# A 31-column loop of fp32 matmuls with its two operands exchanged

## Chip, cores and metric

The kernel runs on one core of a Trainium2 chip. The metric is the device time of one execution in microseconds (us), here the median of several runs of the same program. The engines are TensorE (PE in the profile, with its weight loads on a row of their own, PEld), VectorE (DVE), ScalarE (ACT), GpSimd (POOL) and SyncE (SP), which issues most transfers.

## What is computed

The program is one decoder layer on 512 tokens of width 1024: a norm, one input projection, four groups of attention heads (MoBA, NSA, differential, sliding window), an output projection, a second norm and a gated MLP with a short convolution. The change touches one small part of the NSA group, the compression of keys and values, once for keys and once for values:

```python
def _nsa_compress(x, pos_emb, w1, b1, w2):       # x: (b, 1, 512, 64)
    c = x.reshape(b, g, s // 16, 16, dh)
    nc = c.shape[2] - 1                           # 31 blocks
    win = jnp.concatenate([c[:, :, i:i + nc] for i in range(2)], axis=3)   # 31 blocks of 32 tokens
    hid = jax.nn.gelu(jnp.einsum('bgnld,ldf->bgnf', win + pos_emb, w1) + b1)   # f: 128
    return jnp.einsum('bgnf,fd->bgnd', hid, w2)
```

The first einsum is a product of a 31 x 2048 matrix with a 2048 x 128 matrix, in fp32.

## The kernel before

Most products of the kernel split each fp32 operand in a high part (type fp32r) and a low part and add three products (`mm3`, L404 to L407). The compression instead multiplies plain fp32 tiles: in `fill_nsa` (L676) the loop at L732 and L733 runs 16 matmuls per branch, n = 0 for keys and n = 1 for values, that add up in one PSUM bank ("vb"). The loaded operand is a 128x128 piece of w1 (`w1s[n][:, a, :]`) and the 31 columns of the window tile `xxs[n][:, a, :]` stream past it. The result stands with f on the 128 partitions and the 31 blocks as columns, as `hidden` (L706) wants it: there DVE adds the bias per partition (L711) and makes the arguments of the gelu, ACT takes the tanh (L715), and `hidden2` (L718) finishes the tile `hid[n]`. `compressed` (L746) then multiplies `hid[0]` at L750 and `hid[1]` at L757 with w2, makes the scores of the compressed branch (L783, L784), their softmax, and four transpositions (L817); the first product that uses all this stands at L1059.

The order of work comes from two lists. `everything()` (L895) is a generator of pieces, each some three matmuls of the projections; the attention tasks are a list of events (L1155 to L1191) between which `fill` (L915) advances the generator. Work for ACT, DVE and POOL that belongs to the pieces goes by `later` (L283) in a queue named `side`, of which `advance` (L905) pops one step per piece, two if more than six wait. The bodies `hidden` and `hidden2` are such steps (L739). At the mark "nsa" the queue is emptied (L741), before `compressed` runs with a raised priority (L742). After all this the framework's planner puts each engine's instructions in an order by these priorities and by its own estimates of when an operand is ready; on the chip each engine takes its instructions in that order.

Of the kernel before, what the change touches and what calls it, by code (L numbers as in the profile page):

```python
# [11 lines left out]
F32 = mybir.dt.float32  # L12
BF16 = mybir.dt.bfloat16
F32R = mybir.dt.float32r
AF = mybir.ActivationFunctionType
# [215 lines left out]
def kernel(  # L231
# [6 lines left out]
    vec, act, pool, pe, sp = nc.vector, nc.scalar, nc.gpsimd, nc.tensor, nc.sync  # L238
# [8 lines left out]
    st1 = first_half.enter_context(tc.tile_pool(name="st1", bufs=4))  # L247
# [4 lines left out]
    def nm(s):  # L252
        cnt[0] += 1
        return f"{s}_{cnt[0]}"
# [3 lines left out]
    def bank(tag):  # L258
        if tag == "pv":
            turn[0] ^= 1  # L260
            tag = ("va", "vb")[turn[0]]
        return psum.tile([128, 512], F32, tag=tag, name=nm(tag), bufs=1 if tag[0] == "v" else 2)

    def tt(name, tag="F"):
        return acts.tile([128, S], F32R, tag=tag, name=nm(name), bufs={"F": FB, "M": MB, "H": HB}[tag])

    def tf(name):
        return f32(tt(name))
# [14 lines left out]
    def later(*fs):  # L283
        side.extend(fs)
        asked[0] += len(fs)

    def pop():
        side.popleft()()
        asked[1] += 1

    def flush(mark=None):
        while side and (mark is None or asked[1] < mark):
            pop()
# [76 lines left out]
    ident = cst.tile([128, 128], F32, name="ident")  # L370
# [44 lines left out]
    for n in range(2):  # L415
        ps = bank("sc")
        for _ in range(WARM[n]):
            keep(pe.transpose(ps[:, 0:128], ident, ident))
        if n == 0:
            ps = bank("tr")  # L420
# [39 lines left out]
    def mm_done():  # L460
        marks.append(asked[0])

    def fm_unit():
        w = W.take()
        ps = mm_bank()
        yield from fm_pieces(ps, w, hT, slice(0, S))
        W.free()
        return ps
# [6 lines left out]
    def q_stack(ps, dst, scales, put):  # L475

        ts_ = []

        def hi(a):
            ts_.append(tt("qs"))  # L480
            act.activation(ts_[a][dst[a]:dst[a] + 64], ps[64 * a:64 * a + 64, :], AF.Copy, scale=scales[a])

        def lo(a):
            d = dst[a]
            vec.scalar_tensor_tensor(ts_[a][64 - d:128 - d], ps[64 * a:64 * a + 64, :], scales[a],
                                     f32(ts_[a][d:d + 64]), ALU.mult, ALU.subtract)
            put.append(ts_[a])
        return [lambda: hi(0), lambda: hi(1), lambda: lo(0), lambda: lo(1)]

    def k_stack(ps, dst, kls, put):  # L490


        ts_ = []

        def hi(a):
            d = dst[a]
            ts_.append(tt("kk"))
            act.activation(ts_[a][d:d + 64], ps[64 * a:64 * a + 64, :], AF.Copy)
            act.dma_start(f32(ts_[a][64 - d:128 - d]), f32(ts_[a][d:d + 64]))

        def lo(a):
            d = dst[a]
            pool.memset(f32(kls[a][64 - d:128 - d]), 0.0)
            vec.tensor_sub(kls[a][d:d + 64], ps[64 * a:64 * a + 64, :], f32(ts_[a][d:d + 64]))
            put.append(ts_[a])
        return [lambda: hi(0), lambda: hi(1), lambda: lo(0), lambda: lo(1)]
# [27 lines left out]
    def qscale(m, h, dim):  # L534
        return float(-np.float64(dim) ** -0.5 / np.float64(SLOPES[4 * h + m]))
# [59 lines left out]
    ps = bank("tr")  # L595
# [80 lines left out]
    def fill_nsa():  # L676
        ps = yield from fm_unit()
        kc2, w1s, xxs, hid = [], [], [], []

        def copy(n, ps):  # L680
            kc2.append(tf("kc2"))
            act.activation(kc2[n][0:64, :], ps[64 * n:64 * n + 64, :], AF.Copy)

        def shift(n, ps):
            act.activation(kc2[n][64:128, 0:S - 1], ps[64 * n:64 * n + 64, 1:S], AF.Copy)

        def window(n):
            xx = tf("xx")[:, 0:496].rearrange("p (a n) -> p a n", a=16)
            kv = bass.AP(tensor=kc2[n].tensor, offset=kc2[n].offset, ap=[list(kc2[n].ap[0]), [2, 16], [16, 31]])
            vec.tensor_tensor(xx, kv, par[:, 16 * n:16 + 16 * n].unsqueeze(2).to_broadcast([128, 16, 31]), op=ALU.add)  # L690
            xxs.append(xx)
        for n in range(2):
            w1s.append(vpool.tile([128, 16, 128], F32, tag="v", name=nm("w1")) if n == 0 else None)
        sp.dma_start(w1s[0], w1_k[0].rearrange("(a l) d f -> (l d) a f", l=2))
        for n in range(2):
            later(lambda n=n, ps=ps: copy(n, ps), lambda n=n, ps=ps: shift(n, ps))
        later(lambda: window(0), lambda: window(1))
        mm_done()
        ps = yield from fm_unit()
        kls = [tt("kl"), tt("kl")]  # L700
        nks = []
        later(*k_stack(ps, (0, 0), kls, nks))
        later(lambda: nk.extend(zip(nks, kls)))
        mm_done()

        def hidden(n, ps, b):  # L706
            y = st1.tile([128, 32], F32, tag="y", name=nm("y"), bufs=2)
            u = st1.tile([128, 32], F32, tag="u", name=nm("u"), bufs=2)
            g = st1.tile([128, 4, 32], F32, tag="hid", name=nm("hid"), bufs=2)
            vec.memset(y, 0.0)  # L710
            vec.tensor_scalar(y[:, 0:31], ps[:, 0:31], par[:, b:b + 1], None, ALU.add)  # L711
            vec.tensor_mul(u, y, y)
            vec.tensor_scalar(u, u, 0.044715, 1.0, ALU.mult, ALU.add)
            vec.tensor_mul(u, u, y)
            act.activation(u, u, AF.Tanh, scale=math.sqrt(2.0 / math.pi))  # L715
            hid.append((g, u, y))

        def hidden2(n):  # L718
            g, u, y = hid[n]
            vec.tensor_scalar(u, u, 0.5, 0.5, ALU.mult, ALU.add)  # L720
            vec.tensor_mul(g[:, 0, :], u, y)
            if n == 1:
                for h in range(1, 4):
                    vec.tensor_copy(g[:, h, :], g[:, 0, :])
        for n in range(2):
            ps = yield from fm_unit()
            later(*q_stack(ps, (0, 0), [qscale(1, 2 * n + a, 64) for a in range(2)], nq))
            mm_done()
            while len(xxs) <= n:
                pop()  # L730
            ps = bank("vb")
            for a in range(16):  # L732
                pe.matmul(ps[:, 0:31], w1s[n][:, a, :], xxs[n][:, a, :], start=a == 0, stop=a == 15)  # L733
                if a % 3 == 2:
                    yield 1
            if n == 0:
                w1s[1] = vpool.tile([128, 16, 128], F32, tag="v", name=nm("w1"))
                sp.dma_start(w1s[1], w1_v[0].rearrange("(a l) d f -> (l d) a f", l=2))
            later(lambda n=n, ps=ps: hidden(n, ps, 32 + n), lambda n=n: hidden2(n))  # L739
        yield "nsa"  # L740
        flush()  # L741
        with tc.high_priority(HC):  # L742
            compressed(hid)
        yield "cmp"
# [150 lines left out]
    def everything():  # L895
        yield from fill_moba()
        yield from fill_nsa()
        yield from fill_diff()
        yield from fill_swa()
        yield from fill_out()  # L900
# [585 lines left out]
```

## Time and profile before

| | us |
|---|---|
| median of 3 runs | 814.3 |
| lowest and highest of them | 813.13, 814.61 |
| the profiled execution | 814.86 |
| its span, first to last instruction | 813.0 |
| PE busy in it | 776.9 (96%) |
| DVE busy in it | 658.4 (81%) |
| ACT busy in it | 439.2 (54%) |

Busy time is the sum of the spans of an engine's instructions; PE's instructions are pipelined, so a PE that is busy all the time can still be slower or faster at its work. What a matmul costs in a stream is therefore read from the distance between starts, not from its own duration. The granted clock (PEclk) is a share of 2.4 GHz; 0.50 is 1.2 GHz.

### The profile page before, as it was taken

How to read it: one execution, taken by the hardware profiler on the slowest of the kernel's cores; microseconds unless marked ns; L12 is line 12 of the kernel's file. 1: busy time of each engine (PE TensorE's matmuls, PEld its weight loads, DVE VectorE, ACT ScalarE, POOL GpSimd, SP SyncE). 2: the span in 40 equal slices, each digit the busy share in tenths (PEclk: the TensorE clock that was granted, in tenths of full speed). 3: DMA queues.
4: the chain of work that ended last, by engine and by line, in shares of the span. 5: the costliest groups of instructions: out<-in, count | busy, mean ns of one | idle time of the engine just before them, and what ended most of it. 6: DMA issues, size and time to landing. Idle time of an engine off the chain costs nothing.

```text
span 813.0 us, 13542 instructions
## 1 busy us (share of the span) xinstructions
PE 776.9 (96%) x5087; PEld 710.5 (87%) x5087; DVE 658.4 (81%) x1119; ACT 439.2 (54%) x919; POOL 339.2 (42%) x313
## 2 busy tenths in 40 slices
PE   8999999999988688999999999999999999999995
PEld 8998988998867488988998998998997998998984
DVE  5657678678695999995888797897797897989857
ACT  6657566677685535654645354454354454445532
POOL 5245333437255767323533433442361561563102
PEclk9999999999999879999999999999999999999998
DMA  7455123635132113331132324315206116033212
GB/s 214 119 152 140 49 66 84 169 116 182 54 94 96 70 53 105 104 105 52 53 118 90 105 72 136 105 33 175 91 14 208 44 62 207 6 99 105 75 56 104
DMA packets 74457, 80.87 MB, mean 99 GB/s; under 512 B 8294, under 2 KB 58648, under 8 KB 74392
## 3 DMA queue, kind: packets, MB, share of 16 engines
q1 hardware_dynamic: 72568, 75.81, 30.5%
q10 hardware_dynamic: 1824, 4.20, 1.5%
q8 instruction: 40, 0.66, 0.3%
q14 instruction: 25, 0.20, 0.1%
HBM read 73.71 MB, written 2.10 MB: 93 GB/s over the span
## 4 chain that ended last, share of the span: by engine, by line
PE 63%; DVE 28%; DMA 3%; issue 3%; ACT 2%; POOL 0%; ACTq 0%; DVEq 0%; POOLq 0%; SPq 0%
DVE wu L194 11%; PE mm L405 5%; PE mm L406 5%; PE mm L407 5%; PE tr L406 3%; PE mm L1319 3%; PE mm L1321 3%; PE mm L1320 3%; PE tr L407 3%; DVE y L1369 3%; PE tr L405 3%; PE sc L1319 3%; PE sc L1321 3%; PE sc L1320 3%; PE tr L980 2%
## 5 line engine op out<-in xcount | busy, mean ns | idle before, releaser
L194 DVE TENSOR_TENSOR wu<-pair,wu 128x512 fp32r<-128x512 f32 x188 | 176.2, 972 | 17.4 <-ACT wu L191 17.0
L191 ACT ACTIVATE wu<-pair 128x512 fp32r<-128x512 f32 x188 | 108.5, 622 | 79.2 <-PE sc L1321 21.5
L1321 PE MATMUL mm<-fT,wu 128*128 128x256 f32 x488 | 138.3, 283 | 1.1 <-DVE wu L194 1.1
L1319 PE MATMUL mm<-fT,wu 128*128 128x256 f32 x488 | 138.2, 283 | 0.7 <-ACT mo L1350 0.7
L1320 PE MATMUL mm<-fT,wu 128*128 128x256 f32 x488 | 138.3, 283 | 0.0
L1321 PE MATMUL sc<-fT,wu 128*128 128x256 f32 x392 | 111.2, 284 | 0.0
L1320 PE MATMUL sc<-fT,wu 128*128 128x256 f32 x392 | 111.1, 283 | 0.0
L1319 PE MATMUL sc<-fT,wu 128*128 128x256 f32 x392 | 111.0, 284 | 0.0
L152 ACT ACTIVATE wu<-raw 128x512 fp32r<-128x512 f32 (+2 forms) x126 | 71.2, 610 | 69.5 <-DMA raw<-in_ffn_w_down_dram 36.2
L177 POOL TENSOR_TENSOR sum<-pair 128x512 f32<-128x512 f32 x32 | 47.8, 1497 | 141.8 <-DMA pair<-in_ffn_w_up_dram 65.8
L177 POOL TENSOR_TENSOR pair<-pair 128x512 f32<-128x512 f32 x64 | 104.2, 1640 | 2.0
L177 POOL TENSOR_TENSOR pair<-sum,pair 128x512 f32<-128x512 f32 x32 | 55.8, 1759 | 116.9 <-DVE wu L194 115.0
L157 DVE TENSOR_TENSOR wu<-raw,wu 128x512 fp32r<-128x512 f32 (+2 forms) x96 | 71.7, 764 | 33.0 <-ACT wu L152 32.3
L1321 PEld LDWEIGHTS mm<-fT,wu 128*128 128x128 f32 x488 | 93.6, 192 | 1.6 <-DVE wu L194 1.5
L1319 PEld LDWEIGHTS mm<-fT,wu 128*128 128x128 f32 x488 | 93.6, 192 | 1.2 <-ACT mo L1350 0.9
L1320 PEld LDWEIGHTS mm<-fT,wu 128*128 128x128 f32 x488 | 93.6, 192 | 0.3
L948 POOL TENSOR_SCALAR P<-P,rc 128x128 f32<-128x128 f32 (+2 forms) x80 | 43.2, 559 | 83.4 <-DVE rc L1046 44.6
L1319 PEld LDWEIGHTS sc<-fT,wu 128*128 128x128 f32 x392 | 75.4, 193 | 0.4
L1320 PEld LDWEIGHTS sc<-fT,wu 128*128 128x128 f32 x392 | 75.3, 192 | 0.4
L1321 PEld LDWEIGHTS sc<-fT,wu 128*128 128x128 f32 x392 | 75.3, 192 | 0.0
L956 ACT ACTIVATE P<-P,mn 128x128 f32<-128x128 f32 (+2 forms) x96 | 52.1, 545 | 28.3 <-DVE mn L955 27.9
L157 POOL TENSOR_TENSOR wu<-raw,wu 128x512 fp32r<-128x512 f32 (+2 forms) x30 | 41.7, 1394 | 48.6 <-ACT wu L152 33.9
(321 smaller groups left out, 1944.4 us busy)
## 6 DMA issues: line engine op xcount, KB each, us to landing
pair<-in_ffn_w_gate_dram SPq DMA_DIRECT2D x16, 1024.0 KB, 8.0
pair<-in_ffn_w_up_dram SPq DMA_DIRECT2D x16, 1024.0 KB, 5.4
raw<-in_ffn_w_down_dram SPq DMA_DIRECT2D x32, 512.0 KB, 3.7
raw<-in_w_in_dram SPq DMA_DIRECT2D x14, 512.0 KB, 3.9
raw<-in_w_out_dram SPq DMA_DIRECT2D x8, 512.0 KB, 4.0
dd<-parts SPq DMA_DIRECT2D x48, 64.0 KB, 2.5
raw<-in_w_in_dram SPq DMA_DIRECT2D x10, 256.0 KB, 2.8
x<-in_x_dram SPq DMA_DIRECT2D x4, 512.0 KB, 4.8
```

What stands on the lines that cost most here:

```text
L152: keep(self.nc.scalar.activation(box["h"][:, sl], box["r"][:, sl], AF.Copy))
L157: keep(eng.tensor_tensor(box["l"][:, sl], box["r"][:, sl], f32(box["h"][:, sl]), op=ALU.subtract))
L177: self.nc.gpsimd.tensor_tensor(block(g, out), block(g, a), block(g, b), op=op)
L191: self.nc.scalar.activation(box["h"][g], block(g, src), AF.Copy)
L194: self.nc.vector.tensor_sub(box["l"][g], block(g, src), f32(box["h"][g]))
L405: pe.matmul(o, lh, rh, start=first, stop=False)
L406: pe.matmul(o, lh, rl, start=False, stop=False)
L407: pe.matmul(o, ll, rh, start=False, stop=last)
L956: act.activation(pi, pi, AF.Exp, bias=mn[:, i:i + 1], scale=-1.0, accum_out=sm[:, i:i + 1])
L1319: pe.matmul(o, wh, rh, start=first, stop=False, skip_group_check=True)
L1320: pe.matmul(o, wh, rl, start=False, stop=False, skip_group_check=True)
L1321: pe.matmul(o, wl, rh, start=False, stop=last, skip_group_check=True)
```

## The change

The 16 matmuls of each branch exchange their operands: the 31 columns of the window tile are loaded and the 128 columns of w1 stream. The result stands with the 31 blocks on partitions 0 to 30 and f as 128 columns of the same bank. A new side step, `turned`, ahead of `hidden`, lets ACT copy it to SBUF (tile `hrow`, 31x128) and PE transpose it back into columns 256 to 286 of the bank, from where `hidden` reads on.

```diff
+        def turned(ps):
+            h = st1.tile([32, 128], F32, tag="hrow", name=nm("hrow"), bufs=1)
+            act.activation(h[0:31, :], ps[0:31, 0:128], AF.Copy)
+            pe.transpose(ps[:, 256:287], h[0:31, :], ident[0:31, 0:31])
+
...
             for a in range(16):
-                pe.matmul(ps[:, 0:31], w1s[n][:, a, :], xxs[n][:, a, :], start=a == 0, stop=a == 15)
+                pe.matmul(ps[0:31, 0:128], xxs[n][:, a, :], w1s[n][:, a, :], start=a == 0, stop=a == 15)
...
-            later(lambda n=n, ps=ps: hidden(n, ps, 32 + n), lambda n=n: hidden2(n))
+            later(lambda ps=ps: turned(ps), lambda n=n, ps=ps: hidden(n, ps[:, 256:288], 32 + n), lambda n=n: hidden2(n))
```

## Rows read from the trace of the kernel before

**Rows 1.** Page, parts 1 and 2: busy time of the engines, granted clock by slice

```profile
PE 776.9 (96%) x5087; PEld 710.5 (87%) x5087; DVE 658.4 (81%) x1119; ACT 439.2 (54%) x919; POOL 339.2 (42%) x313
...
PEclk9999999999999879999999999999999999999998
```

**Rows 2.** Busy time by stretch: the projections with attention, and the end of attention

```profile
core 0: us, PE busy (x) PEld busy (x) DVE busy (x) ACT busy (x) POOL busy (x), PEclk, DMA share, GB/s
56.00:223.00 167.00, 167.00 (x942) 146.85 (x942) 121.80 (x330) 112.42 (x288) 73.30 (x89) 0.99 0.37 105
223.00:256.00 33.00, 27.26 (x179) 22.86 (x179) 27.43 (x86) 23.79 (x71) 17.90 (x26) 1.00 0.21 65
```

**Rows 3.** L733's matmuls: ns shortest/median/longest, first and last start

```profile
L733 PE MATMUL vb<-xx,w x64: 189/275/275, 74.9 to 102.4; 128*128 128x31 f32 x64
```

**Rows 4.** Chain of waits around L733: start, us, what

```profile
84.85 2.82 PE vb L733 x26
...
97.17 0.59 PE vb L733 x6
...
99.53 0.86 PE vb L733 x8
100.94 1.71 PE vb L733 x16
```

**Rows 5.** The nearest fp32 products: L1103 streams 2 columns, L1110 128

```profile
L1103 PE MATMUL vb<-pair,tmp x16: 165/251/251, 223.6 to 245.0; 128*128 128x2 f32 x16
...
L1110 PE MATMUL va<-ident,tmp x16: 275/275/375, 228.1 to 250.4; 128*128 128x128 f32 x16
```

**Rows 6.** Timeline of PE, in order of time: start, busy us, what

```profile
70.36 0.40 PE L405 MATMUL mm<-hT,wu 128*128 128x512 f32 x1
...
71.05 0.40 PE L405 MATMUL mm<-hT,wu 128*128 128x512 f32 x1
...
88.47 0.63 PE L1012 MATMUL sc<-kk,qs 128*128 128x128 f32 x2
...
91.82 0.49 PE L980 MATMUL tr<-ident,P 128*128 128x128 f32 x3
...
111.03 0.33 PE L757 MATMUL vb<-w2v,hid 128*128 128x64 f32 x2
...
134.10 0.60 PE L817 MATMUL vb<-ident,cp 128*128 128x128 f32 x4
134.46 0.36 PE L1012 MATMUL sc<-kk,qs 128*128 128x256 f32 x1
...
227.53 0.38 PE L1012 MATMUL sc<-kk,qs 128*128 128x256 f32 x1 [0.31 <-DVE mn L955]
...
228.14 1.16 PE L1110 MATMUL va<-ident,tmp 128*128 128x128 f32 x8
229.05 0.54 PE L991 MATMUL vb<-PT,vd 128*128 128x256 f32 x3
```

**Rows 7.** Busy time by stretch, columns as in rows 2

```profile
640.00:648.00 8.00, 8.00 (x69) 8.00 (x68) 6.98 (x8) 3.37 (x7) 3.25 (x2) 1.00 0.05 12
...
84.69:87.51 2.82, 2.82 (x28) 2.82 (x27) 2.50 (x5) 1.71 (x4) 1.66 (x1) 1.00 0.50 140
88.31:91.70 3.39, 3.39 (x12) 2.78 (x11) 1.45 (x9) 1.21 (x5) 0.00 (x0) 0.50 0.23 72
99.37:102.48 3.11, 3.11 (x32) 3.11 (x31) 3.02 (x7) 1.42 (x5) 1.45 (x2) 1.00 0.02 7
102.00:104.00 2.00, 2.00 (x15) 1.80 (x15) 1.90 (x8) 1.92 (x7) 0.48 (x1) 1.00 0.65 181
```

**Rows 8.** Timeline of ACT: the nearest copy of a small PSUM tile

```profile
107.33 0.20 ACT L753 ACTIVATE ck<-vb 128x32 fp32r<-128x32 f32 x1 [0.31 <-PE vb L750]
```

**Rows 9.** DVE's first and last step of the hidden layer: ns, first and last start

```profile
L711 DVE TENSOR_SCALAR y<-vb,par x2: 240/244/249, 88.0 to 102.8; 128x31 f32<-128x31 f32 x2
...
L721 DVE TENSOR_TENSOR hid<-u,y x2: 192/193/194, 90.1 to 107.3; 128x32 f32<-128x32 f32 x2
```

## The prediction

> **What bounds the kernel now.** First the page's busy shares: PE is busy for 776.9 of 813.0 us, and no other engine comes near it [rows 1]. A share over the whole span says little of one place, so next the busy time by stretch: from 56 to 223 us, where the changed loop lies, PE has no idle time at all, while DVE works for 121.8 and ACT for 112.4 of 167 us [rows 2]. So in this stretch the time is the sum of the distances between PE's starts. What PE saves there reaches the end of the attention, where PE idles for 33.00 - 27.26 = 5.74 us behind the softmax [rows 2]; the softmax steps are tied to PE's own order, so I let a saving pass whole.
>
> Third, the loop itself. The 32 matmuls of L733 are 64 passes in the trace [rows 3]: an fp32 product takes two, each with its own load. The chain of waits has 56 of them in four groups, 2.82 + 0.59 + 0.86 + 1.71 = 5.98 us, 0.107 us each [rows 4]; all 64 are 6.83 us. Columns are not what sets this pace: 31 of them stream, and in both L733 stretches the row of weight loads is busy throughout, 2.82 of 2.82 and 3.11 of 3.11 us [rows 7]. A pass costs one load of 128 columns.
>
> Fourth, the granted clock, which the page shows lower in only a few slices, one of them here [rows 1]. Soon after the first long L733 group it is 0.50, 1.2 GHz, from 88.31 to 91.70 us, with PE busy all the time, and it is 1.00 before [rows 7]. After the second long group it stays at 1.00 [rows 7]. So one of two like stretches is followed by a slow one.
>
> **The change, part by part.** All sums are against the profiled execution, 814.86 us (span 813.0 and 1.86 around it); that is 0.56 above the median of 814.3.
>
> *The passes.* The load shrinks from 128 columns to 31, the stream grows from 31 to 128; the 64 passes stay. The trace has no pass with a 31-column load, so the price is bounded. Above: L1110 streams 128 fp32 columns past a load of 128; eight passes take 229.05 - 228.14 = 0.91 us, 0.114 each [rows 6], and the fp32r products of 256 columns at full clock run at 8.00 / 69 = 0.116 [rows 7]. Does the stream or the load set L1110's pace? The shortest durations are 165 ns at 2 columns, 189 at 31 and 275 at 128 [rows 3, 5]: 110 ns over 126 columns, 0.87 ns a column, 0.11 us for 128. The stream alone would take about as long as the load it replaces. Below: if an fp32 column really streamed at the rate of an fp32r one (0.116 us for 256), a pass would be 0.058 us, and 64 of them 3.7, a gain of 3.1 us. I take 0.112, near L1110, which has this very stream: 64 x 0.112 = 7.17, a loss of 0.34 us (by the near rows between nothing at 0.107 and 0.59 at 0.116).
>
> *The clock.* With 128 columns a pass streams without a pause, and I expect the 1.2 GHz stretch to go. Its worth: from 88.47 to 91.82 us PE does four score products and six products of 512 columns [rows 6]. At full clock four score products take 228.14 - 227.53 = 0.61 and six of 512 columns twice 71.05 - 70.36 = 0.69, so 1.99 in place of 3.35 us [rows 6]. Gain 1.36; at most half of the slow 3.39 us [rows 7], 1.70; at least nothing, if the clock falls as before.
>
> The Trainium skill (TensorE: Matmul & The Clock Gate, Part 1) ties the lower clock to PE having been idle. The trace has PE busy for all of the slow stretch and all of the L733 stretch ahead of it; read as busy share, the rule would give the change nothing here, and the sum would end 1.36 higher.
>
> *The transpositions.* Two on PE. Four of L817 take 134.46 - 134.10 = 0.36, so 0.09 each [rows 6]; two are 0.18, say 0.2. Below: nothing, if they fit under other loads; above, their wait, taken up with the rivals.
>
> *The copies.* Two on ACT of 0.20 us each by the nearest one [rows 8], hidden by ACT's idle time of 55 us in the stretch [rows 2]. If that cover is gone they lie on the path with 0.4 us. The copy waits for the last pass, and behind it in ACT's queue stand softmax exponentials and evictions; around 102 to 104 us ACT is busy 1.92 of 2 us [rows 7], so a stop there is felt by those.
>
> *The chain behind.* DVE's add at L711 comes later by the signal to ACT (0.31), the copy (0.20), the transposition (0.09) and a second signal (0.31): 0.9 us [rows 6, 8]. For keys nothing feels it: `hid[0]` is done by about 90.3 us and is wanted only by `compressed`, after `hid[1]`'s branch has begun. For values L721 starts at 107.3 and L757 at 111.03 [rows 6, 9], a slack over 3 us. DVE's other work would stand behind L711 if that waited, but DVE has 45 us of idle time in the stretch [rows 2]. The bank "vb" is held 0.9 us longer; the next user comes 9 us after L711 has read it [rows 4, 9] and does not notice.
>
> *The order.* Each branch puts one more step in the `side` queue, so the steps behind it, weight splits among them, come one piece of three products later, 0.69 us [rows 6], until the queue is emptied at the mark "nsa". No transfer is added or moved, and neither SP's nor POOL's queue sees a new instruction. I count nothing, and allow 1 us either way for the planner's rearrangement.
>
> Sum: 814.86 + 0.34 + 0.2 - 1.36 = 814.04. **Forecast 814.0 us**, 0.3 below the median shown: no change that a measurement of this kernel can tell, since about 0.2%, 1.63 us, is what it can tell from none.
>
> **Rivals.**
>
> *Cheap stream.* With a short load a 128-column pass costs 0.058 us. Gain 3.1 instead of a loss of 0.34: 814.0 - 3.4 = 810.6. For it: no row has a 31-column load. Against it: the durations [rows 3, 5]. Chance 0.08.
>
> *The clock gives nothing.* Either it falls behind the exchanged loop as it fell behind the old one, or it did not fall in the median execution of the kernel before; the second long group, without a fall, speaks for that [rows 7]. 814.86 + 0.54 = 815.4; against a median without a fall, 814.3 + 0.54 = 814.8. Chance 0.24.
>
> *A wait in PE's queue, the slower end.* PE takes its instructions in order. If the planner puts the transposition close behind the last pass, PE stands from that pass until the copy is there: 0.31 + 0.20 + 0.31 = 0.8 us at least, and up to the 1.92 us of ACT's work in front more at the second loop [rows 7, 8]. Twice 0.8 is 1.6, with ACT's queue 3.5: 815.6 to 817.5, middle 816.6. It decides once fewer than about four products of 512 columns (0.23 each, [rows 6]) stand between last pass and transposition. Against it: PE does not idle once from 56 to 223 us, so the planner finds filler [rows 2]. Chance 0.14.
>
> *Loads that do not hide.* A load of 31 columns is 31/128 of 0.107, 0.026 us; shown in each of 64 passes it adds 1.7: 815.7. The present pace speaks against it, as the loads of 128 columns are already under the streams: 0.116 for 256 columns is no sum of two such times [rows 7]. Chance 0.04.
>
> The Trainium skill (TensorE: Matmul & The Clock Gate, Part 3, The mechanism) says that a load overlaps a running matmul only where they use different rows of the array; by that rule this last rival would hold. The trace disagrees, with 0.116 us for a pair that would otherwise take some 0.21.
>
> **How the numbers follow.** The forecast has 0.50. Its own range is 812.7 to 815.4, from the clock's 1.70, the pass's 0.116 and 1 us of order. Faster by over 0.2% is below 812.67: the cheap stream, 0.08, and 0.10 from the forecast's low side, 0.18 in all. Slower is above 815.93: 0.11 of the wait, 0.02 of the loads, 0.05 of the clock's case with a poor order, 0.18. The same has 0.64. The range 812.2 to 816.6 leaves out the cheap stream and the upper half of the wait, with 0.04 of strays, some 0.19.
>
> **What would show it.** Right: 64 passes of L733 at 0.11 us between starts, the weight-load row no longer full beside them, clock 1.00 from 84 to 104 us, two transpositions of 0.09 with no idle time ahead of them on PE. Wrong: passes well under 0.1 or at 0.13 us, a stretch at 0.50 behind the loop, or PE idle for a releaser on ACT's new line.

## The result, and the profile after

The changed kernel takes 821.0 us, median of 4 runs (820.14 to 822.57), beside 814.45 for the kernel before in the same runs (813.13 to 815.65). The ratio is 1.0083, 95% interval 1.0061 to 1.0105: slower by some 6.7 us, and 4.4 us above the upper end of the wider range that was forecast (816.6). The profiled execution of the changed kernel took 821.01 us, with a span of 819.2.

Line numbers above 706 grow by five: the loop is L738, the new copy on ACT L708, the new transposition on PE L709, the hidden layer's first step L716, the transpositions of the probabilities L985 (before L980), the score products L1017 and L1018 (L1012, L1013), the compressed branch's transpositions L822 (L817).

The page first, parts 1 and 2, where [rows 1] stood before:

```profile
PE 782.9 (96%) x5089; PEld 710.8 (87%) x5089; DVE 654.3 (80%) x1119; ACT 440.3 (54%) x921; POOL 337.8 (41%) x313
...
PEclk9999999999999969999999999999999999999999
```

PE has two instructions more and is busy for 6.0 us more. That is nearly all of the loss, so it lies in PE's pace and not in idle time over the whole span; but busy time hides a slow clock, so the next view is the busy time by stretch (columns as in [rows 2]):

```profile
56.00:223.00 167.00, 164.66 (x914) 141.16 (x913) 115.03 (x319) 109.91 (x282) 70.80 (x89) 0.99 0.37 104
223.00:256.00 33.00, 29.02 (x165) 23.32 (x164) 25.96 (x89) 23.24 (x72) 14.03 (x21) 0.95 0.21 65
...
88.31:91.70 3.39, 3.39 (x22) 2.97 (x22) 0.64 (x4) 1.55 (x6) 0.00 (x0) 1.00 0.16 49
139.62:143.02 3.40, 3.40 (x12) 2.74 (x12) 3.39 (x11) 2.41 (x8) 1.52 (x4) 0.50 0.35 83
132.00:140.00 8.00, 6.10 (x34) 4.70 (x33) 7.63 (x25) 6.12 (x17) 1.00 (x1) 0.98 0.17 42
235.20:238.60 3.40, 3.40 (x13) 2.99 (x12) 1.38 (x6) 2.33 (x9) 3.24 (x5) 0.50 0.48 149
```

From 56 to 223 us PE had no idle time [rows 2]; now it has 2.34 us, and 914 products begin there in place of 942. The slow stretch behind the first loop is gone, as forecast (88.31 to 91.70 at 1.00, was 0.50 [rows 7]). Two new ones stand far behind the loop, at 139.6 and 235.2. And from 132 to 140 us PE works only 6.10 of 8 us. The same stretch of the kernel before:

```profile
132.00:140.00 8.00, 8.00 (x44) 6.85 (x43) 6.03 (x18) 5.27 (x15) 3.36 (x5) 1.00 0.38 92
```

So much of the loss stands far behind the loop. The loop itself, and the new steps behind it, in the views by line:

```profile
L738 PEld LDWEIGHTS vb<-w,xx x64: 104/109/109, 75.0 to 103.6; 128*31 128x31 f32 x64
L738 PE MATMUL vb<-w,xx x64: 272/273/297, 75.0 to 103.7; 128*31 128x128 f32 x64
...
L708 ACT ACTIVATE hrow<-vb x2: 266/266/267, 88.4 to 104.0; 31x128 f32<-31x128 f32 x2
...
L709 PE MATMUL vb<-ident,hrow x2: 243/243/243, 92.1 to 108.6; 31*128 31x31 f32 x2
...
L716 DVE TENSOR_SCALAR y<-vb,par x2: 250/251/252, 92.4 to 108.9; 128x31 f32<-128x31 f32 x2
```

Each copy comes right behind its loop, but each transposition only 3.7 and 4.6 us after its copy, so the values' hidden layer starts at 108.9 in place of 102.8 [rows 9]. That is the planner's choice, not a wait: PE's timeline has other products between, and no idle time in front of L709:

```profile
85.37 3.02 PE L738 MATMUL vb<-w,xx 128*31 128x128 f32 x26
88.33 0.39 PE L996 MATMUL va<-PT,vm 128*128 128x256 f32 x1
...
102.06 1.94 PE L738 MATMUL vb<-w,xx 128*31 128x128 f32 x16
103.92 0.44 PE L1017 MATMUL sc<-kk,qs 128*128 128x384 f32 x1
...
108.27 0.39 PE L406 MATMUL mm<-hT,wu 128*128 128x512 f32 x1
108.59 0.24 PE L709 MATMUL vb<-ident,hrow 31*128 31x31 f32 x1
108.76 0.50 PE L407 MATMUL mm<-hT,wu 128*128 128x512 f32 x1
109.10 0.40 PE L405 MATMUL mm<-hT,wu 128*128 128x512 f32 x1
```

**The place.** The waits of PE from 130 to 146 us, and then the timelines of PE, ACT and DVE around them, one behind the other (start, busy time, what, and in brackets the idle time before it with its releaser):

```profile
PE sc L1017 <- DVE mn L960: 1.9, 2, 1.6
```

```profile
121.60 0.40 PE L407 MATMUL mm<-hT,wu 128*128 128x512 f32 x1
...
135.15 0.39 PE L407 MATMUL mm<-hT,wu 128*128 128x512 f32 x1
...
136.81 0.50 PE L1017 MATMUL sc<-kk,qs 128*128 128x512 f32 x1 [0.27 <-DVE mn L960]
...
139.37 0.39 PE L1017 MATMUL sc<-kk,qs 128*128 128x256 f32 x1 [1.63 <-DVE mn L960]
...
141.31 0.80 PE L405 MATMUL mm<-hT,wu 128*128 128x512 f32 x1
...
133.51 0.64 ACT L805 ACTIVATE cp<-cp 128x512 f32<-128x512 f32 x1 [2.47 <-DVE cp L804]
...
136.94 0.59 ACT L838 ACTIVATE parts<-mm 128x512 fp32r<-128x512 f32 x1
...
140.58 0.67 DVE L844 SCALAR_TENSOR_TENSOR parts<-mm,parts 128x512 fp32r<-128x512 f32 x1
```

Read it from the projection products, the work that fills PE's gaps. They stop at 135.15 and go on at 141.31. The next group needs a bank of "mm", of which there are two. The one that it gets was full with the product at 121.60; it is emptied by L838 on ACT and L844 on VectorE. L838 stands in ACT's order behind L805, the exponential of the compressed branch, for whose input ACT waits 2.47 us; L844 stands behind the whole softmax of that branch on VectorE, ends at 141.25, and the group starts 0.06 us later. In between PE has little but score products left, which wait for VectorE (0.27 + 1.63 us), and behind that wait the granted clock is 0.50 for 3.40 us. The same place in the kernel before, PE, ACT and DVE one behind the other:

```profile
133.87 0.39 PE L407 MATMUL mm<-hT,wu 128*128 128x512 f32 x1
...
135.03 0.48 PE L405 MATMUL mm<-hT,wu 128*128 128x512 f32 x1
...
129.64 0.63 ACT L800 ACTIVATE cp<-cp 128x512 f32<-128x512 f32 x1 [1.19 <-DVE cp L799]
...
130.78 0.57 ACT L833 ACTIVATE parts<-mm 128x512 fp32r<-128x512 f32 x1
...
131.88 0.69 DVE L810 TENSOR_TENSOR cp<-cp,csm 128x512 f32<-128x512 f32 x1
...
133.71 0.68 DVE L839 SCALAR_TENSOR_TENSOR parts<-mm,parts 128x512 fp32r<-128x512 f32 x1
```

Here too the eviction (L833, L839) stands behind the branch's exponential (L800) on ACT and behind its last step (L810) on VectorE, so this place in the queues is not what is new. New is how the two streams of work stand to each other. Before, the bank was full at 126.21 and the next group started at 135.03, 8.8 us later. Now the projections are 4.6 us further ahead, the exponential comes 3.9 us later, and the bank stands full for 19.7 us. The projections pause in the kernel before as well, from 139.37 to 144.68, but PE has other products then and no idle time. No instruction of the change is in this picture: the order of the others is.

### The profile page after: what moved, and what is told of

The parts are those of the page before. It is cut to its first block, busy times and chain, and to the rows that moved or that the text cites. A ratio compares the mean times of both kernels' runs of the same rounds, so it can differ in the third digit from the quotient of the medians.

```text
span 819.2 us, 13540 instructions
## 1 busy us (share of the span) xinstructions
PE 782.9 (96%) x5089; PEld 710.8 (87%) x5089; DVE 654.3 (80%) x1119; ACT 440.3 (54%) x921; POOL 337.8 (41%) x313
## 4 chain that ended last, share of the span: by engine, by line
PE 60%; DVE 30%; issue 3%; ACT 3%; DMA 3%; POOL 1%; ACTq 0%; DVEq 0%; POOLq 0%; SPq 0%
DVE wu L194 11%; PE mm L405 4%; PE mm L406 4%; PE mm L407 4%; PE tr L406 3%; PE mm L1324 3%; PE mm L1326 3%; PE mm L1325 3%; PE tr L407 3%; PE sc L1326 3%; PE sc L1325 3%; PE sc L1324 3%; PE tr L405 3%; DVE y L1374 3%; PE tr L985 2%
## 5 line engine op out<-in xcount | busy, mean ns | idle before, releaser
L157 POOL TENSOR_TENSOR wu<-raw,wu 128x512 fp32r<-128x512 f32 (+2 forms) x30 | 39.7, 1326 | 55.1 <-ACT wu L152 47.0
```

The source lines that it names most:

```text
L157: keep(eng.tensor_tensor(box["l"][:, sl], box["r"][:, sl], f32(box["h"][:, sl]), op=ALU.subtract))
```

## Experiments

Each was timed in five rounds against the kernel before on the same chip. The groups e, p0 to p3, and r with p4 ran on three different chips, so between groups the ratios compare better than the medians. The first four (e1, e2, e3, e5) ask which part of the change costs; each of them got a planned order of its own.

**One branch alone.** Theory A: the transposition puts one more link into the values' chain, holds the bank "vb", and so delays the compressed branch until PE lacks work. Theory B: the exchanged passes cost it. C: any new order of the planner does.

```diff
             for a in range(16):
-                pe.matmul(ps[0:31, 0:128], xxs[n][:, a, :], w1s[n][:, a, :], start=a == 0, stop=a == 15)
+                if n == 0:
+                    pe.matmul(ps[0:31, 0:128], xxs[n][:, a, :], w1s[n][:, a, :], start=a == 0, stop=a == 15)
+                else:
+                    pe.matmul(ps[:, 0:31], w1s[n][:, a, :], xxs[n][:, a, :], start=a == 0, stop=a == 15)
```

The step `turned` is queued for that branch alone. This is the kernel with the keys exchanged; for the values the condition is n == 1.

> Only the keys' loop (n = 0) has its operands exchanged and its result turned back; the values' loop stays as before. Theory A (one more link, on the values' side: the transposition holds the bank vb, so that the first product of the compressed branch, which needs that bank, starts some 5 us later, and the attention behind it stalls): the keys' transposition has more than 10 us of slack, so the time is that of the kernel before, 813 to 815.5 us, and the first product with w2 starts within 2 us of 107. Theory B (the exchanged passes themselves cost the time, half in each loop): some 817.5 us. Theory C (any change of the planner's order costs some us, whatever it is): anything from 812 to 821.

Measured (e1) 813.84 us, ratio 0.9996 (0.9985 to 1.0008): nothing lost, as A has it and B has not.

> Only the values' loop (n = 1) has its operands exchanged and its result turned back. Theory A: the whole loss, 820 to 822.5 us, with the first product with w2 at about 112 us in the trace and PE idle or slow before the compressed branch's transpositions. Theory B: some 817.5 us. Theory C: anything from 812 to 821.

Measured (e2) 817.06, ratio 1.0043 (1.0027 to 1.0059): about half the loss, as B has it; A had nearly all of it.

**The detour without the exchange**: the old loops, then a copy and a product with the identity matrix, so the link is there and the passes are as before.

```diff
+            act.activation(h[:, 0:31], ps[:, 0:31], AF.Copy)
+            pe.matmul(ps[:, 256:287], ident, h[:, 0:31], start=True, stop=True)
...
```

> The loops stay as before (w1 loaded, 31 columns stream); only the detour is added in both: ACT copies the 31 columns to SBUF and PE multiplies them by the identity into columns 256 to 286 of the bank, from where the hidden layer reads on. Theory A: the detour alone gives the whole loss, 819.5 to 823 us. Theory B: 814.3 plus the cost of four small passes and two copies, 814 to 815.5 us. Theory C: anything.

Measured (e3) 813.98, ratio 0.9994 (0.9981 to 1.0006). The compressed branch's transpositions come at 144.2 us here, later than in the changed kernel (140.4), and nothing is lost. Lateness of that branch is not the cost. Nor is a pause of the projections by itself: they stop from 134.37 to 139.01 here, with the eviction (L838 at 135.65) behind the exponential (L805 at 133.44), but PE has other work and waits only 0.3 us in all from 100 to 150.

**The link shortened**: the changed kernel with the two products with w2 on the bank "tr", so that they needn't wait for "vb".

```diff
-        ps = bank("vb")
+        ps = bank("tr")
         pe.matmul(ps[:, 0:32], w2kt, hid[0][0][:, 0, :], start=True, stop=True)
...
```

> The changed kernel, but the two products with w2 write to banks of the tag tr (two buffers) instead of vb, so that they don't wait for the bank that the values' transposition holds. Theory A: the loss goes, 812 to 815.5 us, and the scores of the compressed branch start no later than in the kernel before (116 us). Theory B: 821 us, since the passes are the same. Theory C: anything.

Measured (e5) 829.48, ratio 1.0185 (1.0166 to 1.0205): the transpositions of the compressed branch come at 124.6 us, 16 us earlier than in the changed kernel, and the kernel is 15 us slower than before. With this A falls. Early or late, the time follows neither the branch nor the passes; C is left, that the order itself is what was changed. The change of order is large: of PE's 5037 instructions that the two kernels share, 887 stand at other places in the order of the changed kernel (the lists written into p0 and p1 below).

**Work and order apart.** The order of issue of every engine is written into the program (each instruction is told its predecessor on its engine, which adds no semaphore), so that work and order can be crossed.

```diff
...
         tile_decoder_layer_kernel(tc, *args)
+        _pin(nc, tc)
```

> Control for the next two: the kernel before, with the order of issue that its planner found written into the program for every engine, so that the planner has no choice left. Both theories, order (the loss of the change lies in the order of issue that the planner found for it) and work (it lies in the exchanged passes with their copies and transpositions): as before, 813.5 to 815 us. If it is off by more than 1.5 us, writing the order down costs something by itself, and the next two are read against this one.

Measured (p0) 813.84, ratio 1.0001 (0.9990 to 1.0012). Writing it down costs nothing that can be told.

> The work of the kernel before, to the last instruction, in the order of issue that the planner found for the changed kernel, on all engines; no copy, no transposition, and 31 columns stream as before. Theory order: as slow as the changed kernel, 819 to 822 us. Theory work: as before, 813.5 to 815.5. In between, 816 to 818: the order makes up its share, and the rest is the work.

Measured (p1) 819.96, ratio 1.0075 (1.0060 to 1.0091). **Without one exchanged pass, copy or transposition most of the loss is there**, 819.96 - 813.84 = 6.1 us of it. The same wait, the same full VectorE and the same slow clock, in this kernel's busy time by stretch and waits:

```profile
132.00:140.00 8.00, 6.02 (x27) 4.25 (x26) 8.00 (x29) 6.79 (x22) 1.98 (x4) 0.87 0.21 50
138.01:141.42 3.41, 3.41 (x10) 2.58 (x10) 3.04 (x11) 1.74 (x6) 2.22 (x5) 0.51 0.34 81
```

```profile
PE sc L1012 <- DVE mn L955: 1.9, 2, 1.6
```

> The work of the changed kernel in the order of issue of the kernel before. The two copies and the two transpositions are put in by hand: the copy right behind the loop in the order of ACT, the transposition 8 products behind the loop on PE, and the first steps of the hidden layer on VectorE two or four steps later than they were. Nothing else changes place. Theory order: about what the prediction's sum gave, 814.0 (812.5 to 815.5), with the clock at 1.00 behind the first loop. Theory work: as the changed kernel, 819 to 822.

Measured (p2) 815.87, ratio 1.0031 (1.0021 to 1.0042): 2.0 us above p0. Most of the loss is gone, though less than theory order had it; the work has a price too, above the forecast's.

> The changed kernel with the number that raises the priority of the compressed branch at 30 in place of 50; the same work, and 479 of PE's 5039 instructions stand at other places in the planned order. Theory order: another time than 821, on either side, 812 to 828; it gives no number. Theory work: 819.5 to 822.5.

Measured (p3) 821.43, ratio 1.0096 (1.0081 to 1.0112): as the changed kernel, which is what theory work said and theory order only allowed. The trace is beside it: this order has 479 of PE's instructions elsewhere, but the same pause of the projections (135.19 to 141.49), and the low clock again, from 140.7 us, so the bad place is in this one as well. By itself this run tells nothing apart.

**The place repaired.** In the order of the changed kernel the eviction goes ahead of the exponential, and 15 projection products, which could not start without it, go ahead of the score products that waited. The orders at this place (VectorE's is not shown):

```diff
 ACT   ... L961 exp
+ACT   L838 eviction of the full bank
 ACT   L805 exp of the compressed branch
 ...
 PE    L985 transpositions
+PE    9 projection products
 PE    L1017, L1018 scores (waited 0.27 and 1.63 us)
+PE    6 projection products
```

> The changed kernel in its own order of issue, but for one place: the eviction that frees the bank of the next projection group (L838 on ACT, L844 on VectorE) goes ahead of the compressed branch's exponential on ACT and behind its subtraction on VectorE, and 15 projection products that wait for this bank go ahead of the score products before which PE stood idle. 8 instructions of ACT, 20 of VectorE and 27 of PE change place. Theory place (what the new order loses, it loses mostly at this one place: 0.27 + 1.63 us of waits and a clock at 1.2 GHz from 139.6 to 143.1 that follows them): 816.0 to 818.0 us, no wait of PE over 0.5 us and no low clock before 200 us. Theory spread (the new order is worse all along, VectorE is full there, and a wait that is taken away here comes back a few us later): 819.5 to 822.

> The same repair on the work of the kernel before in the order of the changed kernel, that is on p1 (819.96). Theory place: 815 to 817. Theory spread: 818.5 to 821.

Measured (r1) 818.66, ratio 1.0061 (1.0049 to 1.0073), for the changed kernel: between the two theories. On the old work (r2) 816.65, ratio 1.0035 (1.0022 to 1.0048), 3.3 us below p1: as theory place had it. Busy time by stretch in r1, and its only wait of PE from 130 to 146 us:

```profile
132.00:140.00 8.00, 7.43 (x42) 5.99 (x40) 6.55 (x21) 5.61 (x15) 1.02 (x1) 1.00 0.41 100
140.00:144.00 4.00, 4.00 (x23) 3.13 (x22) 3.88 (x15) 2.58 (x8) 1.70 (x4) 1.00 0.48 119
```

```profile
PE tr L985 <- DVE csm L809: 0.6, 1, 0.6
```

The repair did at its place what it should (waits 1.9 to 0.6 us, 42 products in place of 34, no slow clock), and it takes 3.3 of the order's 6.1 us in r2. In r1 the gain against the changed kernel, about 2 us, is no larger than the two intervals allow for. The order on ACT is also only the last thing that holds the bank: in r1 the eviction, now ahead, still waits 0.65 us for a transfer out of the tile that it writes, and starts at 131.92. The other 2.8 us of r2 lie elsewhere. The traces show a slow stretch from 231 to 234 us in r2 and one from 233.5 to 240.3 in r1, none there in p0; but p2 (235.2 to 238.6) and p4 below have one as well, in the old order, and p4 loses nothing that can be told. One wait before 208 us stands in p1 and r2 and not in p0: 1.0 us of a projection product for L504 on VectorE. No run removes it, so what holds the 2.8 us stays open.

**What the work costs.**

> What in the new work costs the 2 us by which p2 (815.87) is above p0 (813.84), both in the old order? Here the old loops, 31 columns streaming, with the detour alone (two copies, two products with the identity matrix) at the places that they have in p2. Theory edges (the exchanged passes cost it: 0.115 us inside a row of passes, and some 0.1 at each entry and exit of a row): 813.5 to 814.7. Theory detour (the copies and the later hidden layer cost it): 815.2 to 816.5.

Measured (p4) 814.32, ratio 1.0005 (0.9996 to 1.0014): theory edges. The copies and the later hidden layer cost nothing that can be told from none; the exchange holds most of the 2.0 us, 1.6 by the medians (815.87 - 814.32) and 2.1 by the ratios. PE's timeline shows where. The same instructions in p0, then in p2, clock 1.00 in both:

```profile
97.67 1.02 PE L733 MATMUL vb<-xx,w 128*128 128x31 f32 x8
98.53 0.31 PE L980 MATMUL tr<-ident,P 128*128 128x128 f32 x1
98.68 0.31 PE L733 MATMUL vb<-xx,w 128*128 128x31 f32 x2
98.82 0.42 PE L980 MATMUL tr<-ident,P 128*128 128x128 f32 x2
99.08 1.87 PE L733 MATMUL vb<-xx,w 128*128 128x31 f32 x16
100.78 0.42 PE L980 MATMUL tr<-ident,P 128*128 128x128 f32 x2
```

```profile
99.56 1.06 PE L738 MATMUL vb<-w,xx 128*31 128x128 f32 x8
100.56 0.33 PE L985 MATMUL tr<-ident,P 128*128 128x128 f32 x1
100.81 0.41 PE L738 MATMUL vb<-w,xx 128*31 128x128 f32 x2
101.15 0.44 PE L985 MATMUL tr<-ident,P 128*128 128x128 f32 x2
101.52 1.94 PE L738 MATMUL vb<-w,xx 128*31 128x128 f32 x16
103.38 0.44 PE L985 MATMUL tr<-ident,P 128*128 128x128 f32 x2
```

Twenty-six passes with three transpositions between them take 100.78 - 97.67 = 3.11 us with the old operands and 103.38 - 99.56 = 3.82 with the new. Inside a row of exchanged passes one takes 2.96 / 26 = 0.114 us (from 85.37 to 88.33 in the changed kernel) or 1.86 / 16 = 0.116 (in p2), against 0.107 before: 0.2 us for 26. The other 0.5 stands at the places where a pass with 31 loaded columns and a transposition with 128 follow one another, four inside this stretch and one at its end, some 0.1 us each. The other rows of passes stand between products with 128 loaded columns and lose at their ends too: the first, of two passes, takes 0.99 us from the start of the product ahead of it to the start of the second one behind it in p2 (74.83 to 75.82), and 0.68 in p0 (74.53 to 75.21). Counted in this way, all 64 passes cost 2.0 us more in p2 than in p0, some 0.5 of it inside the rows and the rest at their ends.

## Why the prediction was wrong

The step that failed is **the order**: "I count nothing, and allow 1 us either way for the planner's rearrangement". The rearrangement is worth 6.1 us with no change of the work (p1). (The 15 us of e5 were not taken apart, so how much of them is order is not shown.) The reason given was too small: the prediction looked at the `side` queue, where a step comes one piece later, and at nothing else. What the 1 us missed is that the projections, which fill PE, ran ahead of the compressed branch and then stood without a bank, so that PE waited 1.9 us and ran at a clock of 0.50 for 3.4 us behind it; with that place repaired, 3.3 of the 6.1 us go (r2). What in the edit made the planner choose this order no run here shows, and it stays open, as do the other 2.8 us.

The rest, by its steps:

- *What bounds the kernel*: right, and it held the warning. PE without one gap from 56 to 223 us [rows 2] was read as a place where a saving passes whole. It is as much a place that another order can open: the changed kernel's order does, at 6.1 us, while the orders of e1 and e3 lose nothing.
- *The passes*: inside a row the forecast was near, 0.114 to 0.116 us against 0.112. The ends of the rows are missing from the sum, and with them the exchange costs 2.0 us in PE's timeline (1.6 by the medians of p2 and p4) in place of 0.34.
- *The clock*: the stretch at 88.31 is at full clock in the changed kernel and in p2, as forecast. But the gain of 1.36 us can't be counted whole. p0 is the kernel before, to the last place in every order, and in its profile the clock doesn't fall there; r2, with the old loops, falls at 87.73:

```profile
88.31:91.70 3.39, 3.39 (x23) 2.98 (x22) 1.86 (x9) 2.28 (x7) 0.00 (x0) 1.00 0.18 54
```

```profile
87.73:91.12 3.39, 3.39 (x11) 2.83 (x10) 0.87 (x5) 0.99 (x4) 0.00 (x0) 0.51 0.33 103
```

  (p0 first, then r2.) So one profiled execution showed a fall that another with the same instructions in the same order does not have. Of the seven profiled executions with the old keys' loop, two fall behind it; of the six with the exchanged one, none. That is too few to say that the exchange keeps the clock up, and the full clock that was forecast may be luck. The prediction named this as the second half of a rival, that the clock gives nothing; p0 bears that half out.
- *The transpositions*: 0.17 us each between starts (108.59 to 108.76) against 0.09, but their neighbours move apart as well. From 108.27 to 109.10 it is 0.83 us, where two projection products alone take 0.46 (twice 0.23, [rows 6]): 0.37 us of PE's time each, 0.74 for both in place of 0.2. PE did not stand idle in front of them. The rival of a wait in PE's queue did not come: the planner kept 3.7 and 4.6 us between copy and transposition, so PE never stood for the copy.
- *The copies*: 0.27 us against 0.20, hidden (p4).
- *The chain behind*: "0.9 us" was the chain without the planner; it came to 6.1 us for the values. The "9 us" until the next user of "vb" hold for the keys alone: behind the values' L711 at 102.8 the next product into that bank, L750, starts at 107.0. "Does not notice" was right in effect: in e3 the values' hidden layer starts at 106.9, 4.1 us later than in the kernel before, and nothing is lost.
- *Cheap stream* and *loads that do not hide* both fell at 0.114 us. By the Trainium skill (TensorE: Matmul & The Clock Gate, Part 3, The mechanism) a load overlaps a running matmul only where their rows of the array differ, and here they don't. The passes inside a row disagree, as the loads alone last 0.104 to 0.109 us and the passes take 0.114 with 128 columns streaming; the same section also lets a load into a background buffer of weights run ahead, which would fit them, but no run here tells. What is left at the edges, 0.1 us, is about such a load, and no run here shows whether it is one.

Order 6.1 and work 2.0 make 8.1 us, the change lost 6.7. The intervals allow for the difference (1.0060 to 1.0091 and 1.0021 to 1.0042 against 1.0061 to 1.0105); it may also be that in an order that leaves PE waiting some of the work's price is paid out of the waits, which no run here shows.

## What to carry to other kernels

Where a planner orders the instructions, an edit can cost more by the order that it leads to than by its own work: 6.1 us against 2.0 here, and nothing in e1 and e3. So the range for the order must not be a token 1 us, above all where one engine has no idle time that a loss could go into. To learn what an edit itself costs, cross it with the order: the old work in the new order, and the new work in the old one. In a trace, look for a shared bank that stands full while its eviction waits behind another branch's softmax, and look at what PE has left to do meanwhile: the kernel before and e3 have the same order on ACT and lose nothing by it. Exchanging the operands of an fp32 product gained nothing here, where the new stream is as wide as the load that it replaces: 0.114 to 0.116 us a pass against 0.107.

## What was not expected of the hardware

- A row of passes with 31 loaded columns costs at its ends: some 0.1 us at each change to or from a product with 128, while inside the row a pass takes 0.114 us.
- The same instructions in the same order show the clock at 0.50 behind the first loop in one execution (the kernel before) and 1.00 in another (p0). In the changed kernel the low stretch at 139.6 us begins right behind a wait of 1.63 us that ends at 139.37; there the trace fits the Trainium skill (TensorE: Matmul & The Clock Gate, Part 1), which ties the lower clock to PE having been idle. At 88.31 in the kernel before, and at 87.73 in r2, PE was busy throughout, and there it does not. And in the kernel before a wait of 1.59 us ends at 231.65 with the clock at 1.00 from 228 to 236, so a wait of this length is not always followed by a fall.
